# Low halves of split weights: a VectorE subtraction replaced by a ScalarE negation and an adding DMA

## Chip, core and metric

One core of a Trainium2 chip runs the whole kernel. The metric is the device time in microseconds (us), median of the runs shown; the profile is of one execution on the same core.

## What is computed

One layer on 1024 tokens of width 1024, in float32. The weights come as `w_in` (1024 x 10248), `w_pa`, `w_pb` and `w_out` (1024 x 1024 each). Cut to what matters:

```python
h = rmsnorm(x, norm_g)
q, k, v, o_pre, i_pre, f_pre, z_a, glu_in, z_b, ga_pre, gb_pre = split(h @ w_in)
q, k = silu(causal_conv4([q, k]))
hm = rmsnorm_per_head(mlstm(q, k, v, i_pre + b_i, f_pre + b_f)) * mhn_g
y_a = (sigmoid(o_pre) * hm * silu(z_a)) @ w_pa
u = causal_conv31(glu_in[:, :1024] * sigmoid(glu_in[:, 1024:])) + dw_b
y_b = (silu(layernorm(u)) * silu(z_b)) @ w_pb
merged = sigmoid(ga_pre) * y_a + sigmoid(gb_pre) * y_b
out = rmsnorm(x + merged @ w_out) * final_g
```

## The kernel before

**Split operands.** Every float32 operand of a matmul is held as two tiles in TensorE's rounded format `fp32r`: a high half, the rounded value, and a low half, the value less the high half. `mm3` (L152 to L158) then makes a product of three matmuls: high x high, high x low, low x high. `split` (L137 to L140) makes the halves: ScalarE copies the source into the high half (L138), VectorE subtracts that from the source (L139).

**Weight slots.** The weights are cut into 104 slots of 128 x 1024 numbers (128 x 1056 for slots 0 and 1). `do_load(i)` brings slot i from DRAM into a raw tile `wraw` on SP's queue; there are two raw buffers. `do_split(i)` (L142 to L150) makes `whi` and `wlo` from it; there are three buffers of each. A raw buffer is free for the next load when both halves are made; a `whi` or `wlo` buffer is free when TensorE has done the last matmul that reads it. `ahead(i, n)` is called inside item i: it splits slots up to i + n and loads two more.

**Order of the work.** Phase 1 goes through four heads. Each has 14 slots: two for `v`, used together for all token tiles; then two each of `q`, `k`, `o` and `za`, and `gb`, `ga`, `gb`, `ga` of the gated linear unit, a slot an item of 48 matmuls of 512 columns. The mLSTM of the head runs in between the later items. The convolution of 31 taps is done by VectorE at low priority, and GpSimd adds its result to `s1` (L349, L351) and clears the rim of the next `u` (L336), whose buffer it must wait for. Phase 1b has eight slots each of `sg` for the two merge gates and `zb`, then come `yb` and `ya`, again a slot an item. A scheduler puts the instructions of each engine into an order ahead of the run; within an engine they then go in that order.

**Output projection.** The last eight slots, 96 to 103, hold `w_out` by blocks of 256 columns, two slots a block: slot 96 + 2n holds the upper half of the rows of block n, slot 97 + 2n the lower. Block n goes through eight token tiles, and each tile needs 12 matmuls of 256 columns with the first slot and 12 with the second. So both slots of a block are in use until its last tile, and only one buffer is left for the block to come.

```python
for n in range(4):
    for j in range(2):
        do_split(i + j)
    for t in range(TT):
        mm(ps, t, 0, KT)
        if t == 0:
            ahead(i, 2)
```

In the names of the profile a buffer's number is left out: `whi` stands for the high half of any slot. `warm`, `xT`, `v`, `q`, `sg`, `out` are tiles in PSUM by what they hold; `hn`, `rs` and `hth` belong to the normalised input at the start; `res` holds the residual.

Of the kernel before, what the change touches and what calls it, by code (L numbers as in the profile page):

```python
# [9 lines left out]
F32 = mybir.dt.float32  # L10
# [30 lines left out]
def kernel(ctx: ExitStack, tc: tile.TileContext, x, norm_g, w_in, b_if, conv_qk_w, conv_qk_b,  # L41
                      mhn_g, dw_w, dw_b, ln_g, ln_b, w_pa, w_pb, w_out, final_g, out):
    nc = tc.nc
# [21 lines left out]

    # scratch in DRAM
    c_dram = dpool.tile([KT, P, S], F32, name="c_dram")
# [6 lines left out]

    # constants
    ident = cpool.tile([P, P], F32, name="ident")
# [22 lines left out]

    # ---------------------------------------------------------------- weights  # L100
    def w_cm(w, c0):
# [40 lines left out]
    def do_split(i):  # L142
        if i < len(slots) and i not in done:
            done.add(i)
            do_load(i)
            raw, n = raws[i]
            hi = wpool.tile([P, SLOT], F32R, tag="whi", name=f"whi{i}")
            lo = wpool.tile([P, SLOT], F32R, tag="wlo", name=f"wlo{i}")
            split(hi[:, 0:n], lo[:, 0:n], raw[:, 0:n])
            splits[i] = (hi[:, 0:n], lo[:, 0:n])  # L150

    def mm3(ps, pairs, first=True, last=True, lo_last=False):  # L152
        """ps (+)= sum of a^T b over the pairs of split operands."""
        todo = [(a[p], b[q]) for a, b in pairs for p, q in PASSES]
        if lo_last:
            todo = [(a[p], b[q]) for p, q in PASSES for a, b in pairs]
        for j, (a, b) in enumerate(todo):
            nc.tensor.matmul(ps, a, b, start=(first and j == 0), stop=(last and j == len(todo) - 1))  # L158

    # ---------------------------------------------------------------- x -> normalised, transposed  # L160
    ht_cm, ht_pool = pool("ht_pool", side="right", reuse_waits="tile")
# [65 lines left out]

    # ---------------------------------------------------------------- projection pieces
    def proj(i, name, rhs=None):
        """out^T tile [128 channels, 1024 tokens] of one weight slot; yields between quarters of a half."""  # L230
        do_split(i)
        hi, lo = splits.pop(i)
        wv = [v.rearrange("p (k c) -> p k c", k=KT) for v in (hi, lo)]
        ps = pj(name)
        for hf in range(2):
            sl = slice(hf * 512, (hf + 1) * 512)
            pairs = [((wv[0][:, k, :], wv[1][:, k, :]),
                      (hth[:, k, sl], htl[:, k, sl]) if rhs is None else rhs(k, sl)) for k in range(KT)]
            for k in range(0, KT, 2):
                mm3(ps[:, sl], pairs[k:k + 2], first=k == 0, last=k == KT - 2)  # L240
                yield
        return ps

    state = {}

    # ---------------------------------------------------------------- phase 1 pools
    cv_cm, cv = pool("cv", side="right", reuse_waits="tile")
# [49 lines left out]
    def qk_item(i, h, which, j):  # L297
        """which 0: q, 1: k; channel tile j of the head; causal conv of 4 taps and silu."""
        key = ("q", "k")[which]
        if j == 0:  # L300
            state[key] = h1.tile([P, 2, S], F32, tag=key + "raw", name=f"{key}raw{h}")
        acc = state[key][:, j, :]
        ps = yield from proj(i, f"{key}{h}_{j}")
        t = which * 8 + h * 2 + j
        raw = h1.tile([P, S], F32, tag="tmp", name=f"{key}pre{h}_{j}", bufs=TMP)
        nc.scalar.copy(raw, ps)
        nc.scalar.activation(acc, raw, AF.Identity, bias=cb(t), scale=cw(KQ - 1, t))
        for s in range(1, KQ):
            for a, b in ((s, 512), (512, S)):
                nc.vector.scalar_tensor_tensor(acc[:, a:b], raw[:, a - s:b - s], cw(KQ - 1 - s, t), acc[:, a:b],  # L310
                                               op0=ALU.mult, op1=ALU.add)
        nc.scalar.activation(acc, acc, AF.Silu)
# [45 lines left out]

    # ---------------------------------------------------------------- gates of the mLSTM
    def gates():  # L360
# [8 lines left out]
        for j, dst in ((0, ir), (1, fr)):  # L369
            for hf in range(2):  # L370
# [3 lines left out]
                nc.scalar.activation(dst[:, hf * 512:(hf + 1) * 512], ps[0:H, :], AF.Identity, bias=bif[:, j:j + 1])  # L374
        # log sigmoid: min(f, 0) - log1p(exp(-|f|))
        nc.scalar.activation(ab, fr, AF.Abs)
# [40 lines left out]

    # ---------------------------------------------------------------- one chunk of the mLSTM of one head, in stages
    def mlstm(h, c):
# [7 lines left out]
        def prepare():  # L427
# [9 lines left out]
            split(kh, kl, k[:, :, sl])  # L437
            # decay matrix, transposed: [s, t]
            dm = mp.tile([P, 3 * P], F32, tag="dm", name=f"dm{n}")
# [52 lines left out]
        def update():  # L492
            if c < NC - 1:
# [15 lines left out]
                state["C"] = (cf, ch, cl)  # L509
            # normaliser, head norm  # L510
            num = L["num"]
# [31 lines left out]
    def mlstm_events(h):  # L543
        """(step of the head's last eight items, stage); eight steps an item, the output gate done after four."""
        ev = []
        for c in range(NC):
            st = mlstm(h, c)
            b = 13 + 12 * c
            ev += [(1 if c == 0 else b - 10, st[0]), (b, st[1]), (b + 2, st[2]), (b + 6, st[3]), (b + 7, st[4]),
                   (max(b + 13, 37 + 2 * c), st[5])]  # L550
        return deque(sorted(ev, key=lambda e: e[0]))

    # ---------------------------------------------------------------- plan of phase 1
    heads = []
# [66 lines left out]

    # ---------------------------------------------------------------- phase 1b: gates of the merge, layer norm
    p1 = len(slots)
# [8 lines left out]
    def run(gen, i):  # L632
        """drive a projection to its end, the next weights prepared meanwhile."""
        while True:
            try:
                next(gen)
            except StopIteration as e:
                return e.value
            ahead(i, 1)
# [10 lines left out]
    def token_stat(acc, n):  # L650
        """sum over channels of acc, to [128 tokens, 8]."""
        ps = ms(f"tstat{n}")
        for t in range(TT):
            nc.tensor.matmul(ps[:, 2 * t:2 * t + 2], acc[:, t * P:(t + 1) * P], ones, start=True, stop=True)
        st = sgp.tile([P, TT], F32, name=f"tst{n}")
        return ps[:, 0:2 * TT].rearrange("p (t o) -> p t o", o=2)[:, :, 0:1].rearrange("p t o -> p (t o)"), st
# [68 lines left out]

    # ---------------------------------------------------------------- y_b, y_a, merge
    y_cm, yp = pool("yp", side="right", reuse_waits="tile")
# [30 lines left out]

    # ---------------------------------------------------------------- output projection, residual, final norm
    r_cm, rp = pool("rp", side="right", reuse_waits="tile")  # L760
# [83 lines left out]
```

## Time and profile before

| what | us |
|---|---|
| median of 3 runs | 1290.25 |
| lowest and highest run | 1290.05, 1291.18 |
| profiled execution, first to last instruction (span) | 1287.4 |
| TensorE busy | 1275.8 |
| VectorE busy | 816.8 |
| ScalarE busy | 456.6 |
| GpSimd busy | 82.0 |

For the profiled execution only its span is given; the median of the runs lies 2.85 us above it, which is what lies around the first and the last instruction. A row of a timeline gives the start of an instruction in us from the span's start, its duration, its engine (PE is TensorE, DVE VectorE, ACT ScalarE, POOL GpSimd, SPq the queue of SyncE), the line of the kernel, the operation and its tiles; in brackets stands how long the engine was idle before and what released it. Matmuls overlap: the next one starts before the record of the last one ends, so the pace is read from their starts.

### The profile page before, as it was taken

How to read it: one execution, taken by the hardware profiler on the slowest of the kernel's cores; microseconds unless marked ns; L12 is line 12 of the kernel's file. 1: busy time of each engine (PE TensorE's matmuls, PEld its weight loads, DVE VectorE, ACT ScalarE, POOL GpSimd, SP SyncE). 2: the span in 40 equal slices, each digit the busy share in tenths (PEclk: the TensorE clock that was granted, in tenths of full speed). 3: DMA queues.
4: the chain of work that ended last, by engine and by line, in shares of the span. 5: the costliest groups of instructions: out<-in, count | busy, mean ns of one | idle time of the engine just before them, and what ended most of it. 6: DMA issues, size and time to landing. Idle time of an engine off the chain costs nothing.

```text
span 1287.4 us, 16051 instructions
## 1 busy us (share of the span) xinstructions
PE 1275.8 (99%) x6636; PEld 1079.1 (84%) x6636; DVE 816.8 (63%) x1008; ACT 456.6 (35%) x626; POOL 82.0 (6%) x122
## 2 busy tenths in 40 slices
PE   8999999999999999999999999999999999999997
PEld 7888889888889888898888888888888888888997
DVE  6783479995499984799964899262155333344433
ACT  5565441345431444423454211141333211212224
POOL 1000000001000100001010001050000000000002
PEclk9999999999999999999999999999999999999999
DMA  7112121211111221212121123464332344333403
GB/s 219 45 48 53 46 58 42 82 50 58 54 54 50 66 70 37 66 41 66 49 74 50 42 90 115 133 227 127 102 98 82 115 144 137 96 99 98 180 18 132
DMA packets 121495, 109.82 MB, mean 85 GB/s; under 512 B 4945, under 2 KB 109769, under 8 KB 121422
## 3 DMA queue, kind: packets, MB, share of 16 engines
q1 hardware_dynamic: 121422, 108.80, 27.7%
q8 instruction: 52, 0.85, 0.3%
q14 instruction: 21, 0.17, 0.0%
HBM read 87.79 MB, written 21.00 MB: 84 GB/s over the span
## 4 chain that ended last, share of the span: by engine, by line
PE 96%; ACT 1%; DVE 1%; POOL 1%; DMA 0%; issue 0%; SPq 0%; POOLq 0%; ACTq 0%
PE sg L158 14%; PE o L158 7%; PE zb L158 7%; PE k L158 7%; PE ya L158 7%; PE q L158 7%; PE ga L158 7%; PE za L158 7%; PE gb L158 7%; PE yb L158 7%; PE v L158 6%; PE out L158 6%; PE sc L158 2%; PE ip L158 1%; PE up L158 1%; PE np L158 1%
## 5 line engine op out<-in xcount | busy, mean ns | idle before, releaser
L344 DVE SCALAR_TENSOR_TENSOR acc<-u,dww,acc 128x1024 f32<-128x1024 f32 x240 | 307.5, 1307 | 2.9
L138 ACT CAST whi<-wraw 128x1024 fp32r<-128x1024 f32 (+1 forms) x104 | 109.1, 1049 | 372.6 <-PE sg L158 110.6
L139 DVE TENSOR_TENSOR wlo<-wraw,whi 128x1024 fp32r<-128x1024 f32 (+1 forms) x104 | 130.8, 1257 | 78.8 <-ACT whi L138 78.4
L158 PE MATMUL sg<-hth,whi 128*128 128x512 f32 x256 | 101.5, 396 | 0.0
L158 PE MATMUL sg<-hth,wlo 128*128 128x512 f32 x256 | 101.5, 396 | 0.0
L158 PE MATMUL sg<-htl,whi 128*128 128x512 f32 x256 | 100.7, 393 | 0.0
L158 PE MATMUL out<-whi,mrg 128*128 128x256 f32 x512 | 90.8, 280 | 0.0
L158 PE MATMUL ya<-oa,whi 128*128 128x512 f32 x256 | 80.4, 395 | 0.0
L158 PE MATMUL yb<-u,whi 128*128 128x512 f32 x256 | 80.0, 394 | 0.0
L158 PEld LDWEIGHTS out<-whi,mrg 128*128 128x128 f32 x512 | 78.6, 189 | 0.0
L158 PE MATMUL v<-whi,hth 128*128 128x256 f32 (+1 forms) x256 | 71.7, 289 | 2.0 <-ACT hth L138 2.0
L158 PE MATMUL out<-wlo,mrg 128*128 128x256 f32 x256 | 72.0, 281 | 0.0
L158 PE MATMUL v<-whi,htl 128*128 128x256 f32 (+1 forms) x256 | 70.0, 282 | 0.4 <-DVE htl L139 0.4
L158 PE MATMUL v<-wlo,hth 128*128 128x256 f32 (+1 forms) x256 | 69.9, 281 | 0.0
L158 PEld LDWEIGHTS sg<-hth,wlo 128*128 128x128 f32 x256 | 48.3, 189 | 11.9
L158 PEld LDWEIGHTS yb<-u,whi 128*128 128x128 f32 x256 | 48.4, 189 | 11.6 <-DVE u L139 0.3
L158 PEld LDWEIGHTS sg<-htl,whi 128*128 128x128 f32 x256 | 48.0, 187 | 11.7
L158 PEld LDWEIGHTS ya<-oa,whi 128*128 128x128 f32 x256 | 48.0, 188 | 11.4
L158 PEld LDWEIGHTS sg<-hth,whi 128*128 128x128 f32 x256 | 48.1, 188 | 11.0
L158 PE MATMUL ga<-hth,whi 128*128 128x512 f32 x128 | 51.3, 401 | 0.0
L158 PE MATMUL za<-hth,whi 128*128 128x512 f32 x128 | 51.2, 400 | 0.0
L158 PE MATMUL gb<-hth,whi 128*128 128x512 f32 x128 | 50.9, 397 | 0.0
(234 smaller groups left out, 2984.7 us busy)
## 6 DMA issues: line engine op xcount, KB each, us to landing
wraw<-in_w_in_dram SPq DMA_DIRECT2D x80, 512.0 KB, 4.1
ct<-c_dram SPq DMA_DIRECT2D x16, 512.0 KB, 4.6
xt<-in_x_dram SPq DMA_DIRECT2D x8, 512.0 KB, 4.2
oa_dram<-ot SPq DMA_DIRECT2D x16, 256.0 KB, 2.1
c_dram<-acc SPq DMA_DIRECT2D x8, 512.0 KB
sgb_dram<-sg_s SPq DMA_DIRECT2D x8, 512.0 KB, 2.6
sga_dram<-sg_s SPq DMA_DIRECT2D x8, 512.0 KB, 3.0
wraw<-in_w_pb_dram SPq DMA_DIRECT2D x8, 512.0 KB, 4.5
```

The lines of the kernel that those rows point to most:

```text
L138: ins = nc.scalar.copy(hi, src)
L139: nc.vector.tensor_tensor(lo, src, hi.bitcast(F32), op=ALU.subtract)
L158: nc.tensor.matmul(ps, a, b, start=(first and j == 0), stop=(last and j == len(todo) - 1))
L344: nc.vector.scalar_tensor_tensor(acc, u[:, k:k + S], dw(k, c), acc, op0=ALU.mult, op1=ALU.add)
```

## The change

For all slots but the first two ScalarE writes the high half as before, and then the negated high half into the tile of the low half. A DMA issued by GpSimd adds the raw weights to that tile, in place, in SBUF. VectorE no longer takes part. The raw tile is read by the DMA, so its buffer is free when the DMA has landed, and TensorE waits for the DMA where it waited for VectorE.

```diff
--- before
+++ after
@@ do_split @@
             hi = wpool.tile([P, SLOT], F32R, tag="whi", name=f"whi{i}")
             lo = wpool.tile([P, SLOT], F32R, tag="wlo", name=f"wlo{i}")
-            split(hi[:, 0:n], lo[:, 0:n], raw[:, 0:n])
+            if i < 2:
+                split(hi[:, 0:n], lo[:, 0:n], raw[:, 0:n])
+            else:
+                nc.scalar.copy(hi[:, 0:n], raw[:, 0:n])
+                nc.scalar.activation(lo[:, 0:n], hi[:, 0:n].bitcast(F32), AF.Copy, scale=-1.0)
+                nc.gpsimd.dma_start(lo[:, 0:n], raw[:, 0:n], accum_op=ALU.add)
             splits[i] = (hi[:, 0:n], lo[:, 0:n])
```

Some comments were taken out too, so lines after L148 have numbers higher by 5: L158 before is L163 in the change.

The scheduler has put the instructions into another order. The first place is TensorE's entry into block 1 of the output projection (`out1_0` is its token tile 0; slots 98 and 99 are its weights). Before, the end of the first slot's part of tile 0 and what follows:

```order
L158 MATMUL out1_0_9008<-whi98_8863,mrg3_8477 128x256
L158 MATMUL out1_0_9008<-wlo98_8864,mrg3_8477 128x256
L158 MATMUL out1_0_9008<-whi98_8863,mrg3_8477 128x256
L158 MATMUL out1_0_9008<-whi99_9004,mrg4_8543 128x256
L158 MATMUL out1_0_9008<-wlo99_9005,mrg4_8543 128x256
L158 MATMUL out1_0_9008<-whi99_9004,mrg4_8543 128x256
```

In the change the same stretch, and what follows it:

```order
L163 MATMUL out1_0_9106<-whi98_8959,mrg3_8568 128x256
L163 MATMUL out1_0_9106<-wlo98_8960,mrg3_8568 128x256
L163 MATMUL out1_0_9106<-whi98_8959,mrg3_8568 128x256
L163 MATMUL out1_0_9106<-whi99_9101,mrg4_8635 128x256
L163 MATMUL out1_1_9143<-whi98_8959,mrg0_8367 128x256
L163 MATMUL out1_1_9143<-wlo98_8960,mrg0_8367 128x256
```

Tile 0 has had 13 of its matmuls and gives way to tile 1 in front of the first matmul that needs `wlo99`. Tile 1 does the same and gives way to tile 2. The first use of `wlo99` stands here:

```order
L163 MATMUL out1_2_9171<-wlo98_8960,mrg2_8501 128x256
L163 MATMUL out1_2_9171<-whi98_8959,mrg2_8501 128x256
L163 MATMUL out1_2_9171<-whi98_8959,mrg3_8568 128x256
L163 MATMUL out1_0_9106<-wlo99_9102,mrg4_8635 128x256
L163 MATMUL out1_0_9106<-whi99_9101,mrg4_8635 128x256
L163 MATMUL out1_0_9106<-whi99_9101,mrg5_8702 128x256
```

Tile 2 has had 10 matmuls by then, so 36 matmuls of block 1 stand ahead of the first use of `wlo99` where 13 stood before. Blocks 2 and 3 begin in the same way, with slots 101 and 103.

The second place is ScalarE at that boundary (`junk` is the square of `res` for the final norm, `mrg` the merged activations). Before:

```order
L138 CAST whi98_8863<-wraw98_8697 128x1024
L138 CAST mrg7_8741<-sga7_8684 128x512 x2
L798 ACTIVATE junk_8765,fss_8766<-res_8754 128x256 x7
L138 CAST whi99_9004<-wraw99_8867 128x1024
L138 CAST whi100_9033<-wraw100_8869 128x1024
L798 ACTIVATE junk_8765,fss_8766<-res_8754 128x256 x8
```

In the change:

```order
L152 CAST whi98_8959<-wraw98_8792 128x1024
L153 ACTIVATE wlo98_8960<-whi98_8959 128x1024
L138 CAST mrg7_8836<-sga7_8778 128x512 x2
L803 ACTIVATE junk_8860,fss_8861<-res_8849 128x256 x7
L152 CAST whi99_9101<-wraw99_8964 128x1024
L153 ACTIVATE wlo99_9102<-whi99_9101 128x1024
L803 ACTIVATE junk_8860,fss_8861<-res_8849 128x256
L152 CAST whi100_9131<-wraw100_8966 128x1024
L153 ACTIVATE wlo100_9132<-whi100_9131 128x1024
```

Each cast is now followed by the negation into `wlo`, and the cast of slot 99 and its negation stand directly behind each other.

The third place is GpSimd's queue early in the second head, where slots 17 to 20 are the second half of `q`, the two of `k` and the first of `o`. In the change:

```order
L154 DMA wlo17_2110<-wraw17_1924 128x1024
L154 DMA wlo18_2176<-wraw18_1926 128x1024
L341 MEMSET u2_3056 128x30
L354 COPY s1_103<-acc0_1618 128x1024
L154 DMA wlo19_2243<-wraw19_2114 128x1024
L154 DMA wlo20_2309<-wraw20_2180 128x1024
```

Before, `MEMSET u2` and the copy into `s1` had no DMA behind them; now the DMAs of slots 19 and 20 stand behind them.

## Rows read from the trace of the kernel before

**Rows 1.** The page's busy times: us (share of span) xinstructions.

```profile
PE 1275.8 (99%) x6636; PEld 1079.1 (84%) x6636; DVE 816.8 (63%) x1008; ACT 456.6 (35%) x626; POOL 82.0 (6%) x122
```

**Rows 2.** Windows (us; PE, PEld, DVE, ACT, POOL busy, clock, DMA); TensorE's waits (total, times, longest).

```profile
50.00:1190.00 1140.00, 1140.00 (x5569) 949.08 (x5568) 746.34 (x860) 396.29 (x505) 65.52 (x79) 1.00 0.27 80
...
PE xT L202 <- DVE hn L199: 0.7, 1, 0.7
PE v L158 <- DVE htl L139: 0.4, 1, 0.4
```

**Rows 3.** Groups of instructions by line: xcount, busy us, mean ns, idle time before.

```profile
L139 DVE TENSOR_TENSOR wlo<-wraw,whi 128x1024 fp32r<-128x1024 f32 x102 | 128.3, 1257 | 78.8 <-ACT whi L138 78.4
L138 ACT CAST whi<-wraw 128x1024 fp32r<-128x1024 f32 x102 | 107.0, 1049 | 371.3 <-PE sg L158 110.6 <-PE ya L158 65.1 <-PE yb L158 40.5
```

**Rows 4.** Timeline at the start: start us, us, instruction, [idle before, released by].

```profile
18.21 1.22 DVE L139 TENSOR_TENSOR wlo<-wraw,whi 128x1024 fp32r<-128x1024 f32 x1
...
21.24 1.01 ACT L138 CAST hth<-xT 128x1024 fp32r<-128x1024 f32 x1 [1.95 <-PE xT L202]
...
21.28 1.40 DVE L199 SCALAR_TENSOR_TENSOR hn<-xt,rs,ng 128x512 f32<-128x512 f32 x2 [0.73 <-POOL rs L195]
...
22.17 0.63 PE L202 MATMUL xT<-ident,hn 128*128 128x128 f32 x4 [0.72 <-DVE hn L199]
```

**Rows 5.** Chain that ended last: start us, us, what.

```profile
204.17 22.65 PE v L158 x192
...
249.19 22.39 PE k L158 x96
...
739.04 89.52 PE sg L158 x384
```

**Rows 6.** Timeline of ScalarE and VectorE in the gate projections `sg`.

```profile
750.08 1.05 ACT L138 CAST whi<-wraw 128x1024 fp32r<-128x1024 f32 x1 [10.14 <-PE sg L158]
...
752.55 1.21 DVE L139 TENSOR_TENSOR wlo<-wraw,whi 128x1024 fp32r<-128x1024 f32 x1
```

**Rows 7.** Timeline of SP's queue and VectorE in the projections `yb`.

```profile
1080.69 0.38 SPq L103 DMA_DIRECT2D wraw<-in_w_pa_dram  x1
1085.26 0.32 SPq L733 DMA_DIRECT2D sgb<-sgb_dram  x1
...
1089.51 1.23 DVE L736 TENSOR_TENSOR m<-yb,sgb 128x1024 f32<-128x1024 f32 x1 [4.28 <-PE yb L158]
```

**Rows 8.** DMA issues: queue, count, KB each, median us from issue to landing.

```profile
wraw<-in_w_in_dram SPq DMA_DIRECT2D x80, 512.0 KB, 4.1
...
oa_dram<-ot SPq DMA_DIRECT2D x16, 256.0 KB, 2.1
...
sgb_dram<-sg_s SPq DMA_DIRECT2D x8, 512.0 KB, 2.6
```

**Rows 9.** Timeline around the first block boundary of the output projection.

```profile
1211.33 1.05 ACT L138 CAST whi<-wraw 128x1024 fp32r<-128x1024 f32 x1 [0.40 <-PE out L158]
...
1212.41 1.23 DVE L139 TENSOR_TENSOR wlo<-wraw,whi 128x1024 fp32r<-128x1024 f32 x1 [1.02 <-ACT whi L138]
1212.42 0.40 PE L158 MATMUL out<-whi,mrg 128*128 128x256 f32 x2
...
1212.74 1.05 ACT L138 CAST whi<-wraw 128x1024 fp32r<-128x1024 f32 x1 [0.36 <-PE out L158]
```

**Rows 10.** Landing of all transfers of `res`; the windows view, last two columns DMA.

```profile
DMA to landing us min/median/max: 2.6/4.1/8.7
...
1212.00:1235.00 23.00, 23.00 (x197) 23.00 (x197) 8.97 (x18) 6.50 (x19) 0.00 (x0) 1.00 0.15 47
```

**Rows 11.** Timeline of GpSimd, one of its small operations.

```profile
198.75 1.57 POOL L523 TENSOR_TENSOR ssm<-ssm,half 128x2 f32<-128x2 f32 x1
```

**Rows 12.** Timeline of GpSimd where it waited for the convolution.

```profile
247.26 0.12 POOL L336 MEMSET u<- 128x30 f32 x1 [46.67 <-DVE acc L344]
247.33 1.98 POOL L349 COPY s<-acc 128x1024 f32<-128x1024 f32 x1
```

## The prediction

> **What bounds the kernel now.** I read the busy table first [rows 1]: TensorE is busy 1275.8 of 1287.4 us, VectorE 816.8, ScalarE 456.6, GpSimd 82.0. TensorE alone fills the span, so taking work from VectorE shortens nothing unless TensorE waits for that work. Next what TensorE waits for: from 50 to 1190 us it is busy 1140.00 of 1140.00 us, and of its waits at the start the two that end on VectorE add up to 0.7 + 0.4 = 1.1 us [rows 2]. That is the whole of what a lighter VectorE can give; a gain above 0.2% (2.6 us, about what a measurement of this kernel can tell from no change) is not to be had there. The question is therefore whether the low halves now arrive too late for TensorE. For that I read, place by place, how long a weight buffer stands free before its new content is used.
>
> **The change part by part.** *Removed:* 102 subtractions of 1257 ns on VectorE, 128.3 us [rows 3]. By rows 2 they lie beside TensorE's work everywhere but at the start. I count them as 0 elsewhere; the cover is TensorE's own 99%.
>
> *At the start:* the subtraction of slot 2 runs from 18.21 us; behind it on VectorE stands `hn` (21.28), for which TensorE waits 0.72 us at 22.17 [rows 4]. Without those 1.22 us it comes earlier. In its place ScalarE gets a negation before the next eviction of `xT`, in front of which it stood idle for 1.95 us [rows 4], more than the negation lasts. Between 0 and 1.1 us is won; I take 0.5.
>
> *Added on ScalarE:* 102 negations. No such row exists; the nearest one of that size on this engine is the cast, 1049 ns [rows 3], so 1.05 us each, 107 us in all. ScalarE goes from 456.6 to about 564 us, still under half of the span.
>
> *Moved:* the last link of the chain. Before: buffer free, cast, subtraction. Now: buffer free, cast, negation, DMA issued by GpSimd, landing. I call "landing" all that lies between the end of the negation and the moment TensorE may use the tile. Its price is in no row, so what it may take comes first.
>
> *Ordinary slots:* eight `sg` projections take 89.52 us, 11.19 each [rows 5]. There are three buffers, so a slot's cast begins when the projection three before it has ended (the cast at 750.08, released by TensorE) [rows 6] and its weights are needed two projections, 22.4 us, later. Cast, the eviction that stands between, and negation take three times about 1.05 us, 3.2; landing may take 19. The raw buffer is also held until landing instead of until 753.76, the end of the subtraction [rows 6], some 5 us longer; the next load into it takes 4.1 us [rows 8], and its own cast comes over 10 us after that. SP's queue is held up with it: in `yb` the load of `sgb` stands behind a raw load. That raw load was issued at 1080.69 and `sgb` at 1085.26, for a product at 1089.51 [rows 7]. With a landing of 5.2 us the raw load goes out near 1085.4 and `sgb` at 1085.8; with 4.1 us to land [rows 8] it is 0.4 us late, and TensorE goes on meanwhile in the second PSUM buffer, 11.2 us. Cost 0.
>
> *The projections after `v`:* a `v` item uses two slots until its end, so the slot after next is freed only 12 matmuls before that end. 192 take 22.65 us [rows 5], so 12 take 1.4; then one projection of 11.2 us covers it (as half of the 22.39 us of `k` [rows 5]). After cast and negation 10.5 us are left for landing. Cost 0 below that.
>
> *The output projection* is the tight place. Block n uses two slots at once, for all eight token tiles, so the second slot of block n + 1 (99, 101, 103) has its buffer back only in the last tile of block n. In the trace the cast of slot 99 starts at 1211.33 and ends at 1212.38, the subtraction ends at 1213.64 [rows 9]. The last matmul of block 0 starts at 1212.42 (its end releases the cast at 1212.74) [rows 9], and a matmul of this width takes 0.118 us (22.65 / 192, [rows 5]). So block 1 starts at 1212.54, and with the old order, where the 14th matmul is the first with `wlo99`, it is needed at 1214.07: 0.4 us in hand, and TensorE shows no wait. In the new order 36 matmuls stand ahead of it (13 of tile 0, 13 of tile 1, 10 of tile 2): needed at 1212.54 + 36 x 0.118 = 1216.79. The negation ends at 1212.4 + 1.05 = 1213.45. Landing may take **3.3 us**; all beyond it stops TensorE, at each of three block boundaries, and nothing later gives it back.
>
> *The price of landing.* Lower end: 2.6 us, a 512 KB store out of SBUF from issue to landing [rows 8]; no row of that size is quicker. Upper end: 8.7 us, the slowest of the 512 KB transfers in and out of `res` [rows 10]. Between them I build up from the store: 2.6 us; the add reads a second operand, and since 256 KB take 2.1 and 512 KB 2.6 [rows 8], a further pass costs 1.0; GpSimd's own part, the descriptors, I set at 1.6, as long as it took for a power of 128 x 2 numbers (1.57) [rows 11]. Together **5.2 us**, as an estimate, nearer to the store than to `res`, whose eight transfers queue behind each other: around the first boundary the DMA engines are busy for a share of 0.15 alone [rows 10].
>
> The Trainium skill, page "DMA: Bandwidth & Descriptors", section "Anatomy of one DMA — SWDGE (gpsimd) path", gives a copy issued by GpSimd 2.0 us plus its bytes over 436 GB/s; the estimate from it is 3.2 us, and by that the three stalls would vanish (rival 1). The Trainium skill, page "Collectives: The Full Stack", section "The bandwidth ceiling: the fold count and why AG ≠ RS ≠ AR", speaks against the change: an add in the DMA path needs two source reads, which halved the rate there. With the bytes counted twice the estimate is 4.4 us and the sum +2.8. No row of this trace shows either.
>
> **Sum.** 3 x (5.2 - 3.3) = 5.7 us more, 0.5 less at the start: +5.2. The profiled execution has a span of 1287.4 us, so about 1292.6 after. The runs' median lies 2.85 us above that span, time outside it that the change does not touch: 1290.25 + 5.2 = **1295.4 us**.
>
> **Rivals.** *1. Landing is hidden.* If it takes no more than about 4.3 us the stalls add 3.0 us or less and, with the start, the result is within 0.2%; below 3.3 us nothing stalls and the time is 1289.7. For it: stores land in 2.6 us [rows 8], and the DMA engines are free then. Against: GpSimd makes the descriptors, and two operands are read. This is the case on the other side, not slower; 4.3 us of landing decides. Chance 0.20.
>
> *2. The adding DMA is slow,* beyond 8.7 us: over 1290.25 + 16.2 - 0.5 = 1306; from 10.5 us on the projections after `v` (three heads) stall too. At 12 us: 3 x 8.7 + 3 x 1.5 - 0.5 = 30, so 1320. For it: no row shows the adding path. Against: `res` took that long with eight transfers in the queue at once; here there is one. Chance 0.10.
>
> *3. GpSimd's queue.* An adding DMA now stands behind `MEMSET u` and `s1`, which wait for the convolution's last tap. Before, these ran at 247.26 and 247.33 and were done at 249.31 [rows 12]; behind them is the DMA for slot 19, the second half of `k`, which starts 11.2 us after 249.19, at 260.4 [rows 5]. It leaves 11.1 us for a landing of 5.2. VectorE has 14 subtractions (17.6 us) fewer per head, so the taps should end earlier. Were they 10 us later instead, 10 - (11.1 - 5.2) = 4.1 us would be lost at each of eight such places: 1290.25 + 33 + 5.2 = 1328. Chance 0.03.
>
> *4. Faster by over 0.2%* would need waits of TensorE that the list does not have. Chance 0.02.
>
> **The numbers.** The forecast, landing between 4.3 and 8.7 us, has 0.65: 1293 to 1306. With rival 1 the lower end becomes 1289.7; leaving out rivals 2 to 4 leaves 0.15 outside. Range 1289.7 to 1306. Slower: 0.65 + 0.10 + 0.03 = 0.78; same 0.20; faster 0.02.
>
> **What the profile after would show.** VectorE near 690 us, ScalarE near 564 us, TensorE's busy time unchanged. The list of waits should have TensorE waiting three times in `out` for the DMA into `wlo`, about 1.9 us each, near 1216.8, 1241 and 1266 us, and nowhere else after the first 50 us. I am wrong if these waits are absent, if they are longer than 5 us, if TensorE waits for `wlo` in `q`, `k`, `sg` or `yb`, or if the wait is on GpSimd's queue rather than on the DMA.

## The result and the profile after

The changed kernel takes **1300.72 us** (median of 3 runs, 1300.4 to 1304.71) against 1290.25 before: 1.009 times the time before, 95% interval 1.007 to 1.011. It is slower by 10.5 us where the prediction said 5.2; the time lies in its range (1289.7 to 1306) and on its side.

The page of the changed kernel, its busy times and the rows of the new work (xcount, then busy us, mean ns of one, idle time before; of a DMA queue packets, MB, share of 16 engines; of a DMA issue KB each and median us to landing):

```profile
PE 1276.9 (98%) x6636; PEld 1080.1 (83%) x6636; DVE 699.3 (54%) x906; ACT 552.7 (43%) x728; POOL 168.7 (13%) x224
...
q0 software_dynamic: 14688, 53.48, 22.1%
...
L154 POOL DMA_DIRECT2D wlo<-wraw x102 | 87.7, 860 | 882.1 <-ACT wlo L153 800.7
L153 ACT ACTIVATE wlo<-whi 128x1024 fp32r<-128x1024 f32 x102 | 107.6, 1055 | 1.3
...
wlo<-wraw POOLq DMA_DIRECT2D x102, 512.0 KB, 4.6
```

Beside [rows 1] VectorE lost 117.5 us and ScalarE gained 96.1 (foretold were some 127 and 107); TensorE does the same work in 1.1 us more. The 102 negations take 1055 ns each, the casts of [rows 3] 1049. Away from the three block boundaries none of that is on the path. What TensorE waits for in the changed kernel (total us, times, longest):

```profile
PE out L163 <- DMA wlo<-wraw: 5.2, 3, 2.2
PE v L163 <- ACT hth L138: 2.0, 1, 2.0
```

There are three waits for the DMA, all in `out`, as foretold. At the start the two waits of [rows 2] are gone or smaller; the 2.0 us of `v` for ScalarE's `hth` are no news, the kernel before has them too (2.0, once). The chain that ended last in the changed kernel, from the first boundary on (start us, us, what):

```profile
1190.02 21.10 PE out L163 x179
...
1213.70 5.34 DMA wlo<-wraw
...
1219.08 17.16 PE out L163 x143
...
1238.82 4.56 DMA wlo<-wraw
...
1243.42 17.30 PE out L163 x144
...
1263.18 4.77 DMA wlo<-wraw
...
1267.99 1.57 PE out L163 x11
1269.59 0.43 DVE res L802
...
1290.38 0.49 POOL frs L810
...
1291.53 0.61 ACT res L813
```

And the same chain before:

```profile
1190.09 70.84 PE out L158 x600
...
1260.95 0.44 DVE res L797
...
1281.86 0.49 POOL frs L805
...
1283.02 0.61 ACT res L808
```

Read the two columns of starts against each other. Up to 1190 the changed kernel is 0.07 us *ahead*: the whole loss comes after it. When the first tile of the last block is finished (`DVE res`) it is 8.64 us behind, at the last `res` 8.51. But TensorE's last matmul ends only 5.9 us later (1286.65), by these two rows, the first from before, the second from the change:

```profile
1280.42 0.28 PE L158 MATMUL out<-whi,mrg 128*128 128x256 f32 x1
...
1286.37 0.28 PE L163 MATMUL out<-whi,mrg 128*128 128x256 f32 x1
```

(The list of waits has 5.2, since there a wait begins only when the record of the last matmul ends, after the next would have started.) And the span is 11.1 us longer (1298.5 against 1287.4), so another 2.6 us come after the last instruction. Three terms, then: **5.9 us of stalls, with the small gain at the start already taken off, 2.7 us in the closing work of the last block, 2.6 us at the program's end**; 0.1 is made up on the way from the first closed tile to the last. The prediction has only the first.

The closing work, ScalarE in the last block of the changed kernel (timeline; in brackets the idle time before and its releaser):

```profile
1272.95 0.40 ACT L803 ACTIVATE junk<-res 128x256 f32<-128x256 f32 x1
...
1274.70 1.15 ACT L813 ACTIVATE res<-res,frs 128x1024 f32<-128x1024 f32 x1 [1.26 <-POOL frs L811]
1275.76 0.40 ACT L803 ACTIVATE junk<-res 128x256 f32<-128x256 f32 x1
...
1277.51 1.15 ACT L813 ACTIVATE res<-res,frs 128x1024 f32<-128x1024 f32 x1 [1.25 <-POOL frs L811]
```

`junk` of a tile goes to GpSimd (`frs`), which releases the scaling `res`, behind which stands `junk` of the *next* tile: a closed circle of 2.81 us a tile. TensorE makes a tile in 2.83 us. Before, tile 0 of the last block was done after 24 matmuls of that block. In the new order 36 matmuls go ahead and 11 more finish tile 0, so it is done after 47: 23 x 0.118 = 2.7 us later beside the stall. A circle as slow as its feeder never catches up.

### The profile page after: what moved, and what is told of

Read it like the earlier page. It is cut to its first block, busy times and chain, and to the rows that moved or that the text cites. A ratio compares the mean times of both kernels' runs of the same rounds, so it can differ in the third digit from the quotient of the medians.

```text
span 1298.5 us, 16324 instructions
## 1 busy us (share of the span) xinstructions
PE 1276.9 (98%) x6636; PEld 1080.1 (83%) x6636; DVE 699.3 (54%) x906; ACT 552.7 (43%) x728; POOL 168.7 (13%) x224
## 3 DMA queue, kind: packets, MB, share of 16 engines
q0 software_dynamic: 14688, 53.48, 22.1%
## 4 chain that ended last, share of the span: by engine, by line
PE 94%; DMA 2%; issue 1%; ACT 1%; POOL 1%; DVE 0%; SPq 0%; POOLq 0%; ACTq 0%
PE sg L163 14%; PE o L163 7%; PE zb L163 7%; PE k L163 7%; PE ya L163 7%; PE q L163 7%; PE ga L163 7%; PE za L163 7%; PE gb L163 7%; PE yb L163 7%; PE v L163 7%; PE out L163 4%; PE sc L163 2%; PE ip L163 1%; PE up L163 1%
## 5 line engine op out<-in xcount | busy, mean ns | idle before, releaser
L152 ACT CAST whi<-wraw 128x1024 fp32r<-128x1024 f32 x102 | 106.8, 1047 | 345.1 <-PE sg L163 96.0
L154 POOL DMA_DIRECT2D wlo<-wraw x102 | 87.7, 860 | 882.1 <-ACT wlo L153 800.7
L153 ACT ACTIVATE wlo<-whi 128x1024 fp32r<-128x1024 f32 x102 | 107.6, 1055 | 1.3
L163 PE MATMUL sg<-hth,whi 128*128 128x512 f32 x256 | 101.6, 397 | 0.0
L163 PE MATMUL sg<-hth,wlo 128*128 128x512 f32 x256 | 101.5, 397 | 0.0
L163 PE MATMUL sg<-htl,whi 128*128 128x512 f32 x256 | 100.8, 394 | 0.0
L163 PE MATMUL out<-whi,mrg 128*128 128x256 f32 x512 | 90.9, 281 | 0.0
L163 PE MATMUL ya<-oa,whi 128*128 128x512 f32 x256 | 80.4, 395 | 0.0
L163 PE MATMUL yb<-u,whi 128*128 128x512 f32 x256 | 80.0, 394 | 0.0
L163 PEld LDWEIGHTS out<-whi,mrg 128*128 128x128 f32 x512 | 78.7, 189 | 0.0
L163 PE MATMUL out<-wlo,mrg 128*128 128x256 f32 x256 | 72.1, 283 | 5.2 <-DMA wlo<-wraw 5.2
L163 PE MATMUL v<-whi,hth 128*128 128x256 f32 (+1 forms) x256 | 71.8, 290 | 2.0 <-ACT hth L138 2.0
L163 PE MATMUL v<-wlo,hth 128*128 128x256 f32 (+1 forms) x256 | 70.2, 283 | 0.0
L163 PE MATMUL v<-whi,htl 128*128 128x256 f32 (+1 forms) x256 | 69.8, 282 | 0.2 <-DVE htl L139 0.2
L163 PEld LDWEIGHTS sg<-hth,wlo 128*128 128x128 f32 x256 | 48.4, 189 | 11.8
L163 PEld LDWEIGHTS yb<-u,whi 128*128 128x128 f32 x256 | 48.4, 189 | 11.6 <-DVE u L139 0.3
L163 PEld LDWEIGHTS sg<-htl,whi 128*128 128x128 f32 x256 | 48.1, 188 | 11.7
L163 PEld LDWEIGHTS ya<-oa,whi 128*128 128x128 f32 x256 | 48.1, 188 | 11.3
L163 PEld LDWEIGHTS sg<-hth,whi 128*128 128x128 f32 x256 | 48.1, 188 | 10.9
L163 PEld LDWEIGHTS out<-wlo,mrg 128*128 128x128 f32 x256 | 48.2, 188 | 5.9 <-DMA wlo<-wraw 5.9
L163 PE MATMUL ga<-hth,whi 128*128 128x512 f32 x128 | 51.4, 401 | 0.0
```

The source lines that it names most:

```text
L152: nc.scalar.copy(hi[:, 0:n], raw[:, 0:n])
L153: nc.scalar.activation(lo[:, 0:n], hi[:, 0:n].bitcast(F32), AF.Copy, scale=-1.0)
L154: nc.gpsimd.dma_start(lo[:, 0:n], raw[:, 0:n], accum_op=ALU.add)
```

## The experiments

Each ran in the same job as the kernel before, whose median there was 1290.0 to 1290.5 us. "End" is the time from the end of the last ScalarE instruction to the end of the span: 3.8 us before (1283.63 to 1287.4), 6.4 in the full change (1292.14 to 1298.5).

### Which slots cost

```diff
-            if i < 2:
+            if i < 2 or i in (99, 101, 103):
```

> Slots 99, 101 and 103 go back to VectorE's subtraction, the other 99 keep the accumulating DMA. My theory splits the 11.1 us that the span grew into three: 5.9 us of TensorE's stalls at the three block boundaries of the output projection, 2.7 us because tile 0 of the last block ends 23 matmuls later in the new order and the serial closing chain (junk, frs, res) cannot make that up, and 2.6 us after the last output store, at the program's end, which a program with DMAs issued by GpSimd pays once. Here the first two go and the third stays: about 1292.8 us, TensorE shows no wait for the DMA into wlo, and the time from the end of the last ScalarE instruction to the span's end is about 6.4 us (3.8 before). Rival A, everything comes from the three boundaries and the end is a consequence of them: 1290.2 us. Rival B, the other 99 DMAs cost something of their own (traffic, queues): 1295 us or more.

Measured: **1291.85 us** (1.0012, interval 1.0003 to 1.0021). TensorE has no wait for a DMA, and goes through 600 matmuls of `out` in 70.84 us as before:

```profile
1189.71 70.84 PE out L163 x600
```

The end takes 6.1 us. The start is 0.4 us ahead of before (1189.71 instead of 1190.09 at the first matmul of `out`). So 1.9 us in the profile, 1.55 in the medians. Rival A falls, if by a small margin, since the end stays long without a late last block; rival B falls too.

```diff
-            if i < 2:
+            if i not in (99, 101, 103):
```

> Only slots 99, 101 and 103 are formed by the accumulating DMA. My theory: these three carry the whole loss, so as slow as the full change, 1300.7 us (1299.5 to 1302), with three waits of TensorE for the DMA into wlo of about 2.2, 1.4 and 1.7 us. Rival B (the 99 others cost something of their own, or delay these three): below 1298 us. A wider gain by the freed VectorE, which this kernel gives up, would show as a time above 1301 us.

Measured: **1300.88 us** (1.0081, 1.0067 to 1.0095), with three waits of 5.3 us together. Three DMAs of 102 make a kernel as slow as the full change. But not all by my reasons: its end takes 3.8 us, not 6.4. That its profiled execution (1299.53 us) is only 0.9 below that of the full change (1300.4) is so because its last ScalarE instruction ends 1.8 us later (1293.93). Most of that lies behind the first stall (windows; the column ahead of the last two is the granted clock):

```profile
1218.00:1220.00 2.00, 1.06 (x9) 1.00 0.77 263
1220.00:1222.00 2.00, 2.00 (x13) 0.60 0.80 250
1222.00:1224.00 2.00, 2.00 (x12) 0.55 0.04 13
1224.00:1226.00 2.00, 2.00 (x19) 1.00 0.00 0
```

TensorE makes 13 and 12 matmuls in 2 us instead of 19: its granted clock fell to about half, the lower of its two levels, for some 3.5 us after it had stood still for 1.9 us. 143 matmuls to the next stall took 18.71 us here, 17.16 in the profile of the full change. So that the two times agree is in part chance: this kernel has no long end, and in its profiled execution lost time to the clock instead.

### One boundary less

```diff
-            if i < 2:
+            if i < 2 or i == 103:
```

> As the full change, but slot 103, the second slot of the last block, is subtracted on VectorE, so that only two boundaries stall and the last block is multiplied in the order of before, 24 matmuls a tile. My theory: the third stall (1.9 us with the restart) and the late closing chain (2.7 us) go, the other two stalls (4.0 us) and the program's end (2.6 us) stay: about 1296.2 us. Rival D, the closing chain costs nothing of its own and only the stall goes: 1298.8 us. In the trace the last matmul and the last frs should be about as far apart as before (1280.4 to 1281.86, 1.5 us), not 4.1 us as in the full change.

Measured: **1296.19 us** (1.0045, 1.0031 to 1.0059), as the theory had it; rival D's 1298.8 is out. The last matmul starts at 1286.57, the last `frs` at 1288.02, 1.5 us apart as before. One slot of 104 is worth 4.5 us, of which the stall is 1.9. (The profiled execution, 1298.2 us, is the longest of its five, with the clock at 0.51 for 3 us behind the first stall.)

### What sets the program's end

```diff
-            if i < 2:
+            if i != 50:
```

> Only slot 50, in the middle of the program, is formed by the accumulating DMA; 101 slots are subtracted on VectorE. My theory: one such DMA is enough for the 2.6 us at the program's end, so about 1292.9 us, with some 6.4 us from the last ScalarE instruction to the span's end. Rival A (the end is a consequence of the late last block) and rival C (the end grows with the number of such DMAs): 1290.3 us, 3.8 us at the end.

Measured: **1290.22 us** (0.9999, 0.9990 to 1.0008), end 3.8 us. My theory of a price paid once falls.

```diff
-            if i < 2:
+            if i < 2 or i > 52:
```

> Accumulating DMA for slots 2 to 52 only (51 of them), VectorE's subtraction from slot 53 on, so no stall at the boundaries. Open is what sets the 2.6 us that the full change has after its last output store and the kernels with 1 and 3 such DMAs have not. Growth with the number (25 ns for each): 5.1 us from the last ScalarE instruction to the span's end, about 1291.5 us. A fixed cost once many are used: 6.3 us, 1292.5 us. Only DMAs near the end count: 3.8 us, 1290.2 us.

Measured: **1290.01 us** (0.9996, 0.9988 to 1.0005), end 4.4 us. In time that is the third form; in the length of the end it is none of the three: 51 DMAs add 0.6 us, 102 add 2.6. Windows over the end, of the full change:

```profile
1292.00:1294.00 2.00, 0.00 (x0) 0.00 (x0) 0.08 (x1) 0.14 (x1) 0.00 (x0) 0.50 0.52 213
1294.00:1296.00 2.00, 0.00 (x0) 0.00 (x0) 0.00 (x0) 0.00 (x0) 0.00 (x0) 0.50 0.13 51
1296.00:1298.50 2.50, 0.00 (x0) 0.00 (x0) 0.00 (x0) 0.00 (x0) 0.00 (x0) 0.50 0.01 3
```

The last store has moved its data by 1294.5, and for 4 us no engine shows work; only a few KB still move. The queue of instruction packets `q14` has 23 packets in all kernels with 99 DMAs and more (24 in one), 22 with 51, 21 with 0, 1 and 3. That suggested a longer instruction stream on GpSimd, whose last part is fetched late:

```diff
+            if i >= 2:
+                nc.gpsimd.memset(idle, 1.0)
+                nc.gpsimd.memset(idle, 1.0)
             splits[i] = (hi[:, 0:n], lo[:, 0:n])
```

> The kernel before, unchanged in its work and without a single DMA from GpSimd, but with 204 idle MEMSETs of one column on GpSimd, two for every slot from 2 on. The program's end took 3.8 us with 0, 1 and 3 adding DMAs, 4.4 with 51, and 6.1 to 6.4 with 99 to 102, and only those with 99 or more show two more instruction packets at the end of the span. If it is the length of GpSimd's instruction stream that makes its last part be fetched late, this kernel shows 6 us or more at the end and about 1292.8 us. If it is the DMAs that GpSimd issues, 3.8 us and 1290.3 us.

Measured: **1298.88 us** (1.0070, 1.0057 to 1.0082), and for neither reason. The loss is at the start, where the idle MEMSETs delay GpSimd's `rs`:

```profile
PE xT L206 <- DVE hn L203: 9.9, 4, 5.4
```

The end takes 3.8 us, although `q14` shows 23 packets. The length of the stream in instructions alone is not it. But a late fetch is not ruled out: these MEMSETs wait for nothing, and all 204 were done by 39.9 us, so that no packet of `q14` comes after 1285 us here, while in the full change one comes between 1296 and 1297. What the runs show is that the long end belongs to kernels in which GpSimd issues many DMAs; 102 copies leave 8.5 us at the end when GpSimd issues them and 3.65 from SyncE's queue (both below). Whether their number counts or their place wasn't tested, as the 51 all lay in the first half. The cause stays open.

### What the landing is made of

```diff
-                nc.gpsimd.dma_start(lo[:, 0:n], raw[:, 0:n], accum_op=ALU.add)
+                nc.gpsimd.dma_start(lo[:, 0:n], raw[:, 0:n].bitcast(F32R))
```

> The full change with the same DMAs from GpSimd, but without the add: they overwrite the tile with the raw weights instead of adding to it (the subtraction is left out). TensorE's order is the same. The prediction counted 1.0 us of the landing for the second operand that the add reads. If so, landing falls from 4.6 to 3.6 us, each stall by 1.0 us to about 1.2, 0.4 and 0.7, and the time to about 1297.5 us. Rival F, the add costs nothing beside GpSimd's own path: landing 4.6 us, 1300.7 us. The program's end (6.3 us after the last ScalarE instruction) should stay.

Measured: **1299.52 us** (1.0077, 1.0059 to 1.0095). The stalls fall from 5.2 to 2.3 us (two instead of three), the last ScalarE instruction ends 3.2 us earlier, at 1288.98, as expected, but the end grew again, to 8.5 us, so that the time is 2.0 us above the 1297.5. The DMA rows of this kernel:

```profile
q0 software_dynamic: 14688, 53.48, 11.5%
...
wlo<-wraw POOLq DMA_DIRECT2D x102, 512.0 KB, 3.0
```

Same bytes, half the engine time: 22.1% of 1298.5 us for 102 adds is 2.81 us each, 11.5% of 1297.5 is 1.46. The Trainium skill, page "Collectives: The Full Stack", section "The bandwidth ceiling: the fold count and why AG ≠ RS ≠ AR", says of a ReduceScatter that its add needs two source reads, and that this makes it half as fast as a plain copy; this pair of rows agrees (1.9 times the engine time). From issue to landing the add takes 4.6 us, the copy 3.0, as medians of all 102. At the three boundaries, where TensorE waits, the add took 5.3, 4.6 and 4.8 us in the full change and the copy 4.5, 2.9 and 4.1: there the second operand costs about 1.1 us, near the 1.0 of the prediction, and not 1.6.

```diff
-                nc.gpsimd.dma_start(lo[:, 0:n], raw[:, 0:n], accum_op=ALU.add)
+                nc.sync.dma_start(lo[:, 0:n].bitcast(F32), raw[:, 0:n])
```

> As the copy without the add, but issued by SyncE's queue instead of GpSimd's (the subtraction is left out). If GpSimd's part of the landing is the 1.6 us of the prediction, landing falls to about 2.6 to 3 us, the like of a store, and TensorE's stalls at the boundaries vanish or are below 0.5 us. If the transfer itself is what takes the time: 3.6 us or more. The program's end should be the 3.8 us of before, since GpSimd issues no DMA: together about 1290 to 1292 us. SyncE's queue order differs, so that its time is weighed less than its landing.

Measured: **1295.22 us** (1.0041, 1.0025 to 1.0057), end 3.65 us. From SyncE's queue:

```profile
wlo<-wraw SPq DMA_DIRECT2D x102, 512.0 KB, 2.9
```

So by the medians GpSimd's queue costs 0.1 us beside SyncE's, not 1.6. But the stalls did not vanish, and the time missed the 1290 to 1292 expected: two are left, of 2.8 us together. At these two boundaries the copies took 4.28 and 5.17 us, at the one without a stall 2.9. Windows over the third boundary of the copy from GpSimd, which was issued at 1260.70 and lets TensorE go on at 1264.84 (second column from the end: DMA share):

```profile
1261.50:1263.25 1.75, 1.75 (x18) 1.75 (x17) 0.02 (x1) 0.00 (x0) 0.00 (x0) 1.00 0.80 286
1263.25:1264.50 1.25, 0.62 (x6) 0.41 (x4) 0.00 (x0) 0.00 (x0) 0.00 (x0) 1.00 0.06 20
```

Nearly all of it has moved by 1263.25; then a share of 0.06, what one engine of 16 makes, goes on for over a microsecond, and TensorE waits until it is over. That one late engine holds up the landing is read from this share; it isn't shown, nor is why it should be late there.

### Mending the two known terms

```diff
@@ output projection, blocks 1 to 3 @@
+        else:
+            for t in range(4):
+                pss[t] = ms(f"out{n}_{t}")
+                mm(pss[t], t, 0, 4)
         for t in range(TT):
             if t in pss:
                 ps = pss[t]
-                mm(ps, t, KT - 1, KT)
+                mm(ps, t, KT - 1 if n == 0 else 4, KT)
```

> The full change, and in blocks 1 to 3 the first four token tiles are multiplied with the first slot only (48 matmuls) before the second slot is used, so that 49 matmuls instead of 36 stand ahead of the first use of the late wlo: 1.5 us more in hand. My theory: the stalls shrink from 2.2, 1.4 and 1.7 us by 1.5 each, to 0.7, 0 and 0.1; the last block starts 3.6 us earlier, its tile 0 ends no earlier relative to that start (60 matmuls instead of 47 and a stall), the closing chain keeps its pace: about 1297 us. Rival E, the landing is late by contention that moves with the use: the stalls stay, 1300.7 us or more.

Measured: **1296.20 us** (1.0043, 1.0030 to 1.0056), a little better than the 1297 of the theory. Weight loads wait 0.8 us for the DMA in three places, the longest 0.4; the last matmul starts at 1282.32, the last ScalarE instruction ends at 1288.06, 5.5 us after TensorE, as the closed circle would have it.

```diff
@@ last block @@
-                cut = 384 if t == TT - 1 else D
-                nc.scalar.activation(res[:, t, 0:cut], res[:, t, 0:cut], AF.Copy, scale=st)
-                if cut < D:
-                    nc.vector.tensor_scalar(res[:, t, cut:D], res[:, t, cut:D], st, None, op0=ALU.mult)
+                cut = 384 if t == TT - 1 else 0
+                if cut:
+                    nc.scalar.activation(res[:, t, 0:cut], res[:, t, 0:cut], AF.Copy, scale=st)
+                nc.vector.tensor_scalar(res[:, t, cut:D], res[:, t, cut:D], st, None, op0=ALU.mult)
```

> The full change, but in the last block the final scaling of res runs on VectorE (of the last tile ScalarE keeps its 384 columns); TensorE's order is the same. My theory: the 2.7 us of the late last block are lost because junk of tile t+1 stands behind res of tile t on ScalarE, a closed chain of 2.81 us a tile, which is TensorE's own pace, so a late tile 0 stays late. With the scaling off ScalarE the chain is open, the end follows TensorE's last matmul (1286.65 end) by 3.1 us as before, instead of 5.5: 2.3 us less, about 1298.4 us. Rival D, the end is late for another reason than this chain: 1300.7 us.

Measured: **1300.51 us** (1.0082, 1.0069 to 1.0095): no gain, as rival D has it. Before believing that, look at VectorE in this kernel:

```profile
1276.91 0.75 DVE L815 TENSOR_SCALAR res<-res,frs 128x1024 f32<-128x1024 f32 x1 [0.80 <-POOL frs L811]
1277.58 0.42 DVE L802 TENSOR_TENSOR res<-out,res 128x256 f32<-128x256 f32 x1
...
1279.86 0.75 DVE L815 TENSOR_SCALAR res<-res,frs 128x1024 f32<-128x1024 f32 x1 [0.80 <-POOL frs L811]
1280.53 0.42 DVE L802 TENSOR_TENSOR res<-out,res 128x256 f32<-128x256 f32 x1
```

The scaling of a tile now stands ahead of the *opening* instruction of the next tile on VectorE. The circle was moved, not opened: 2.95 us a tile. This experiment could not tell the theories apart, and the next one, which has the same edit, could not either.

> Both edits together: four tiles ahead in blocks 1 to 3, and the final scaling on VectorE. My theory: TensorE ends near 1281.7 us, the last ScalarE instruction 3.1 us later, and the program's end takes its 6.3 us: a span of 1291.1 us, about 1293.3 us, of which 2.6 us are the program's end and some 0.9 us stalls. If the closing chain did not matter it would be no better than with four tiles ahead alone, about 1297 us.

Measured: **1295.94 us** (1.0041, 1.0027 to 1.0054), not 1293.3. What was missing is an order in which nothing of tile t + 1 stands behind the close of tile t. The next kernel has the four tiles ahead, and:

```diff
@@ last block @@
-            nc.scalar.activation(junk, r, AF.Square, accum_out=ss[:, t, n:n + 1])
+            sq = nc.scalar.activation(junk, r, AF.Square, accum_out=ss[:, t, n:n + 1])
...
-                cut = 384 if t == TT - 1 else D
-                nc.scalar.activation(res[:, t, 0:cut], res[:, t, 0:cut], AF.Copy, scale=st)
+                for c in ([t - 1] if t else []) + ([t] if t == TT - 1 else []):
+                    cs = rs[:, c:c + 1]
+                    cut = 384 if c == TT - 1 else D
+                    with tc.issue_after(sq.ins):
+                        nc.scalar.activation(res[:, c, 0:cut], res[:, c, 0:cut], AF.Copy, scale=cs)
...
```

> As with four tiles ahead, and in the last block the scaling and store of tile t are issued after junk of tile t+1, so that no tile's opening work stands behind the closing work of the one before it on ScalarE. With the scaling moved to VectorE the chain had closed again there (2.95 us a tile, res of tile t+1 behind the scaling of tile t), so that run could not tell. My theory: the chain now needs 1.65 us of ScalarE a tile against TensorE's 2.83, catches up, and the last ScalarE instruction ends about 2.8 us after TensorE's last matmul (1282.6 in the kernel with four tiles ahead, where it ended 5.5 us after): 2.7 us less than that kernel's 1296.2, so 1293.5 us, up to 1294.1 if the last two stores share the DMA engines. Rival D, the lateness of the last block is not from this chain: 1296.2 us.

Measured: **1293.44 us** (1.0026, 1.0015 to 1.0036), against 1293.5 expected. ScalarE in its last tiles:

```profile
1280.22 0.42 ACT L807 ACTIVATE junk<-res 128x256 f32<-128x256 f32 x1 [1.25 <-DVE res L806]
...
1280.64 1.14 ACT L820 ACTIVATE res<-res,frs 128x1024 f32<-128x1024 f32 x1
1283.02 0.42 ACT L807 ACTIVATE junk<-res 128x256 f32<-128x256 f32 x1 [1.25 <-DVE res L806]
```

`junk` is now released by VectorE, that is by TensorE's tile, and ScalarE is idle before it instead of before `res`. The last ScalarE instruction ends at 1285.40, 2.9 us after the last matmul's end, and the span at 1291.8. The circle was the cause of the second term. What is left of the loss in this kernel is the end (6.4 us, 2.6 more than before) and some 1.0 us for which weight loads wait for the DMA in `out`. No version here is faster than the kernel before: the change offers TensorE at most the 1.1 us of waits at the start, and where all slots but a few go by the DMA the end alone takes 2.3 to 2.6.

## Why the prediction was right, and where its sum fell short

**What bounds the kernel:** right. With TensorE at 99% [rows 1] the lighter VectorE gave nothing; with 99 adding DMAs and no stall the time was 1291.85.

**Ordinary slots, the projections after `v`, GpSimd's queue (rival 3):** right at 0. There is no wait of TensorE for `wlo` outside `out`, and 51 adding DMAs in the first half changed the time by nothing that can be told. In `yb` the raw load and `sgb`, foretold for 1085.4 and 1085.8, went out at 1085.41 and 1085.89.

**The output projection:** right in place, count and size. Foretold were three stalls of 1.9 us from a landing of 5.2 us, at 1216.8, 1241 and 1266. The trace shows TensorE standing still from 1216.9, and in all 5.9 us later at its last matmul, 1.97 a boundary. At the first boundary the negation ended at 1213.40 and TensorE went on at 1219.08, 5.7 us; at the third 1262.88 and 1267.99, 5.1.

**The price of landing:** its sum was right, its parts were not, and that they made up for each other is luck. At the three boundaries the copy from GpSimd took 3.8 us on average, from SyncE's queue 4.1, and the add 4.9. So the base, counted 2.6 us (a store), is 3.8; GpSimd's part, counted 1.6, is 0.3 from the negation to the issue and behind it nothing that can be told; the second operand, counted 1.0, is 1.1. Together 5.2; from the negation's end to TensorE's next matmul the three boundaries show 5.7, 4.9 and 5.1. Each of these is one profile with three boundaries that differ by up to 2.3 us, so the parts are rough.

**At the start:** the 0.5 us were 0.1 in the full change (1190.02 against [rows 5]'s kernel at 1190.09) and 0.4 in the first experiment; executions differ there by more, 1189.71 to 1191.05 over the experiments with the change in its full width.

**The step that failed** is that of the sum: all that comes behind the stalls was left at nothing, with no more said of it than "nothing later gives it back". Nothing gave it back; but something later *added* to it, twice. First, the 36 matmuls that the prediction itself counted ahead of the first use of `wlo` also push the end of tile 0 back, and in the last block that tile starts a circle as slow as TensorE: 2.7 us, shown by its vanishing with slot 103 (4.5 us for one slot, of which the stall is 1.9) and with the opened circle (2.8 us between two medians; in the profiles ScalarE's end 2.9 us after TensorE's instead of 5.5). Second, the program's end: 2.6 us. No row before could tell of it, but "time outside it that the change does not touch" was said of the wrong stretch: what grew lies inside the span, after the last store. It is shown to go with many DMAs from GpSimd, and its cause is open. So the side was right by the mechanism that was forecast, but that mechanism is about half of the loss, and the time lies in the range because the range was made wide for a slower landing, not for these two terms. The 2.85 us between span and median were too much as well: where an execution's own time is known it lies 1.8 to 2.1 us above its span, so the profiled execution before was about 1 us quicker than the median, and 11.1 us of span became 10.5 of median.

**The rivals:** rival 1 fell, as no boundary came down to a landing of 4.3 us; rival 2 too, the slowest add took 10.4 us but not at a boundary. By the Trainium skill, page "DMA: Bandwidth & Descriptors", section "Anatomy of one DMA — SWDGE (gpsimd) path", the estimate of the landing was 3.2 us; that agrees with the copy's median (3.0), and the add takes 4.6.

## What to carry to other kernels

When a change makes a scheduler put other work ahead of a late operand, follow that work to its own end too: ask which tile now finishes later, and whether the chain behind it is faster than what feeds it, since a chain of equal pace keeps every delay. To open such a chain it is not enough to move an instruction to an idler engine: no engine may hold the next tile's first instruction behind this tile's last. And price a DMA that adds as two reads, and take its landing at the very place where it is waited for: at the boundaries the copies took 2.9 to 5.2 us, where their medians were 2.9 and 3.0.

## What was not expected of the hardware

- After a stall of about 2 us TensorE's granted clock fell, in some executions, to the lower level: 0.60 and 0.55 in two windows of 2 us in the kernel with three adds, 0.51 over 3 us in the one with slot 103 on VectorE. 143 matmuls then took 18.7 us instead of 17.16, so a stall can cost 1.5 us more than its length. In the profile of the full change three such stalls left the clock at 1.00. Its longest run, 1304.71 us, has the lowest mean clock of the three (0.994, against 0.996 and 0.997); whether a drop of this kind made it long no trace shows.
- A program in which GpSimd issues some 100 DMAs ends 2.3 to 2.6 us later after its last ScalarE instruction (6.1 to 6.4 us instead of 3.8), with 51 it is 0.6, with 1 or 3 nothing; with 102 plain copies in place of the adds it was 4.7 us (8.5).
- 512 KB within SBUF take the DMA engines 1.46 us as a copy and 2.81 as an add. From issue to landing a copy took 2.9 us at one block boundary and 5.2 at another; in the window that was looked at a share of 0.06 of the engines went on for 1.25 us after the rest had moved.
